# Attention scores from split queries and keys: three fp32r products in place of one float32 product

## The chip, the core and the metric

The kernel runs on one core of one Trainium2 chip. The metric is device time in microseconds (us) of one execution. The engines are named as in the profile: PE (TensorE matmuls), PEld (its weight loads), DVE (VectorE), ACT (ScalarE), POOL (GpSimd), SP (SyncE, which issues the loads).

## What is computed

A two-layer decoder trunk on 512 positions of width 1024: a state-space layer, a feed-forward layer, one attention layer with 16 heads, a second feed-forward layer, all in float32. The change touches the scores of the attention layer only. Keys and queries of a head have 96 entries (64 without and 32 with rotary position). From the reference:

```python
def causal_block_attention(q, k, v):
    ...
    scale = 1.0 / math.sqrt(dk)
    ...
        s = jnp.einsum('bhqd,bhkd->bhqk', q_blk, k).astype(jnp.float32) * scale
        query_pos = blk_idx * Q_BLOCK + jnp.arange(Q_BLOCK)
        s = jnp.where(key_pos[None, :] <= query_pos[:, None], s, NEG_INF)
        p = jax.nn.softmax(s, axis=-1).astype(v.dtype)
        return jnp.einsum('bhqk,bhkd->bhqd', p, v)
```

## The kernel before

The activations lie transposed in SBUF. Almost all matrix products are made by `mm3` (L150): each operand is a pair, a high part in the type float32r and the float32r rest, and three products (high x high L153, high x low L154, low x high L155) are summed in PSUM. `split` (L165) makes such a pair: ACT writes the high part (L168, or L171 with a scale per partition), then DVE subtracts it from the source to give the low part (L169, or L172). Weights are split in the same way (`weights`: ACT L141, DVE L142).

The attention (`attention`, L846) works on quarters of four heads. For each quarter, `open_quarter` (L859) loads and splits the weights, `proj_q` and `proj_kv` (L882, L869) project one block of 128 positions each, and `close_q` and `close_k` (L911, L908) rotate and normalise: four rotary products on DVE, a reciprocal root by eleven small DVE operations on each of two tiles, then the scaling of the queries by DVE and POOL and of the keys by POOL. The helper `tt` is recorded as L853.

For each head, `turn` (L923) transposes the queries or the keys on PE (L927) and copies the result out of PSUM by ACT with a gain per partition (L929), as plain float32 tiles `qT` and `kT` of 96 x 512. `scores` (L932) makes four blocks of 128 queries against 128, 256, 384 or 512 keys, each with one plain float32 product (L942, recorded as two matmuls with two weight loads) and one bf16 product that adds the causal mask (L943). The softmax is the row maximum on DVE (L945), the exponential with its sum on ACT (L947), the reciprocal on DVE (L948) and the scaling by DVE (widest block) or POOL (L950). `turn_p` (L954) transposes the probabilities on PE (L959) and copies them out by DVE or ACT (L964, L966), and `values` (L972) multiplies two heads by their values (L979) and splits the result.

PSUM has four banks `a` for projections and transposes (three from head 9 on), three `s` for the scores, one `po`. The program text runs the heads in a pipeline: the scores of head h+1, the transposes of head h+2 and the projections of the quarter that comes next stand beside the softmax of head h. The final order on each engine is set by a scheduler when the kernel is built (`TCARGS`, L76), from its own estimates of durations; each engine then takes its instructions in that order.

The sums of squares of the compressed latents are kept by `sumsq` (L253); its tile for the latents comes from a pool of intermediate results (L789).

Of the kernel before, what the change touches and what calls it, by code (L numbers as in the profile page):

```python
# [7 lines left out]
F32 = mybir.dt.float32  # L8
F32R = mybir.dt.float32r
BF16 = mybir.dt.bfloat16  # L10
I32 = mybir.dt.int32
AF = mybir.ActivationFunctionType
# [4 lines left out]
P = 128  # L17
D = 1024
S = 512
# [3 lines left out]
T = 4  # L23
# [55 lines left out]
def places(z):  # L79

    return z.rearrange("p (i c) -> p i c", i=T)


def by_place(z):

    return z.rearrange("p (c i) -> p i c", i=T)


class Trunk:
# [160 lines left out]

        return [self.hp.tile([P, S], F32R, name=f"{name}{x}{k}", tag=f"h{x}{k}") for x in "hl"]

    def sumsq(self, k, src=None, acc=None, n="acc", pool=None, natural=False):  # L253
        nc = self.nc
        src = self.x[:, k, :] if src is None else src
        sq = (pool or self.hp).tile([P, S], F32, name=n) if k == 0 else self.hp.tile([P, S], F32, name="sq", bufs=2)
        if natural:
            nc.scalar.activation(out=by_place(sq), in_=places(src), func=AF.Square)  # L258
        else:
            nc.scalar.activation(out=sq, in_=src, func=AF.Square)  # L260
        if k == 0:
            return sq
        nc.gpsimd.tensor_tensor(out=acc, in0=acc, in1=sq, op=ALU.add)  # L263
        return acc
# [469 lines left out]
    def mla(self):  # L734
        tc, nc, a = self.tc, self.nc, self.a
# [7 lines left out]
        with ExitStack() as st:  # L743
            self.banks(a=4, po=1, s=3)
            hs, acc = self.normed(None, "m", natural=True)
            lp = st.enter_context(tc.tile_pool(name="mlal", bufs=1))
            self.qp = st.enter_context(tc.tile_pool(name="mlaq", bufs=2))
            ip = st.enter_context(tc.tile_pool(name="mlai", bufs=1))
# [12 lines left out]
            for w in ("q", "k"):  # L761
                gn = self.s(w + "rope")
                for n, tab, half in (("c1", cs, 0), ("s2", sn, 1), ("s1", sn, 0), ("c2", cs, 1)):
                    z = lp.tile([P, 4, 16], F32, name=f"rt{w}{n}")
# [9 lines left out]
            sacc = {}  # L774
            kr_raw = ip.tile([32, S], F32, name="krraw")
            specs = [(n, m) for n, nt in (("kr", 1), ("kv", 2), ("q", 3)) for m in range(nt)]
            def project(group):
                ws = [self.weights(a["w_" + n + "_a"][m], (KD, 32 if n == "kr" else P), self.s("mix1" if n == "q" else "kvin")) for n, m in group]
                pss = [self.ps("a") for _ in group]
                self.products([ps[0:32] if n == "kr" else ps for ps, (n, m) in zip(pss, group)], ws, hs, len(group) > 1)  # L780
                for ps, (n, m) in zip(pss, group):
                    if n == "kr":
                        nc.scalar.activation(out=by_place(kr_raw), in_=places(ps[0:32]), func=AF.Copy)
                        continue
                    ch = lp.tile([P, S], F32R, name=f"{n}h{m}")
                    cl = lp.tile([P, S], F32R, name=f"{n}l{m}")
                    self.split(by_place(ch), by_place(cl), places(ps), self.s(n + "a")[:, m:m + 1])
                    low.setdefault(n, []).append((ch, cl))
                    sacc[n] = self.sumsq(m, ps, sacc.get(n), n + "acc", ip, natural=True)  # L789

            def columns(z):
                cps = self.ps("s")
# [4 lines left out]
            def factors(j, n, dim):  # L797
# [6 lines left out]
                for i, hd in ((0, 64),) if j == 0 else ((1, 64), (2, 32)):  # L804
                    v.scalar_tensor_tensor(out=tfs[:, i], in0=tf[:, j], scalar=1.0 / hd, in1=tf[:, j], op0=M_, op1=M_)

            project(specs[:2])
            project(specs[2:3])
            rs = lp.tile([P, 4], F32, name="rs")
            self.rsqrt(ip, rs, columns(acc), 1.0 / D, "r1")  # L810
# [5 lines left out]
            for z in specs[3:]:  # L816
                project([z])
# [28 lines left out]
    def attention(self, low, krot, tabs, tf, tfs, maskb, identb):  # L846
        tc, nc, a = self.tc, self.nc, self.a
# [7 lines left out]
        qp = self.qp  # L855
        os = []
        quarters, heads, outs = {}, {}, {}
# [65 lines left out]
        def turn(h, w):  # L923
            z = quarters[h // 4][3 if w == "q" else 2]
            ps = self.ps("a")
            for b in range(4):
                nc.tensor.transpose(out=ps[0:96, b * P:(b + 1) * P], in_=z[:, b, h % 4, :], identity=ident)  # L927
            o = qp.tile([96, S], F32, name=w + "T")
            nc.scalar.activation(out=o, in_=ps[0:96], func=AF.Copy, scale=self.s(w + "nope")[0:96, 0:1])  # L929
            heads[h, w] = o  # L930

        def scores(h):  # L932
            qT, kT = heads[h, "q"], heads[h, "k"]
            mx = qp.tile([P, 4], F32, name="mx")
            sm = qp.tile([P, 4], F32, name="sm")
            pbs = [None] * 4
            b2 = self.ps("s")
            for i in (0, 2, 1, 3):
                n = (i + 1) * P
                bank = b2 if i in (0, 2) else self.ps("s")  # L940
                ps = bank[:, 384:512] if i == 0 else bank[:, 0:n]
                nc.tensor.matmul(out=ps, lhsT=qT[:, i * P:n], rhs=kT[:, 0:n], start=True, stop=False)  # L942
                nc.tensor.matmul(out=ps[:, i * P:n], lhsT=identb, rhs=maskb, start=False, stop=True)  # L943
                m1, s1 = mx[:, i:i + 1], sm[:, i:i + 1]
                v.reduce_max(out=m1, in_=ps, axis=AX.X, negate=True)  # L945
                pb = qp.tile([P, n], F32, name=f"p{i}")
                nc.scalar.activation(out=pb, in_=ps, func=AF.Exp, bias=m1, accum_out=s1)  # L947
                v.reciprocal(out=s1, in_=s1)  # L948
                eng = v if i == 3 else g
                eng.tensor_scalar(out=pb, in0=pb, scalar1=s1, scalar2=None, op0=M_)  # L950
                pbs[i] = pb
            heads[h, "p"] = pbs
# [42 lines left out]
        for h in range(2):  # L995
            turn(h, "q")
            turn(h, "k")
        scores(0)
        for h in range(H):
            nq, nb = divmod(h + 7, 4)  # L1000
            if h + 1 < H:
                scores(h + 1)
            if h + 2 < H:
                turn(h + 2, "q")
# [27 lines left out]
        for m in range(KD):  # L1032
            w, ps = early[m] if m < 1 else (self.weights(a["w_o"][m], (KD, P), pieces=2 if m in (3, 4) else 1), self.ps(("", "s", "s", "a", "a", "a", "s", "a")[m]))
# [102 lines left out]
```

## Time and profile before

| | |
|---|---|
| median of 3 runs | 1246.48 us (1244.24 to 1248.38) |
| the profiled execution: its time | 1248.45 us |
| its span in the trace | 1246.7 us |
| PE busy | 1190.2 us, 95% of the span |
| DVE busy | 673.0 us, 54% |
| ACT busy | 477.9 us, 38% |
| POOL busy | 150.4 us, 12% |

Busy times of PE are overlapping records of pipelined matmuls, so a busy PE isn't a PE at its peak. What a matmul costs is read from the start of one to the start of the next. Idle time of an engine matters where another engine waits for what it does next. The attention stretch on which the change bears runs from about 699 us to 850 us of the span.

### The profile page before, as it was taken

The numbers are of one execution on the slowest core, as the hardware profiler recorded it, in microseconds if no ns is written. First come the engines' busy times: TensorE is split into PE (matmuls) and PEld (weight loads), VectorE is DVE, ScalarE is ACT, GpSimd is POOL, SyncE is SP. The second block draws the span as 40 slices with busy tenths as digits, with TensorE's granted clock in tenths as the row PEclk, the third lists the DMA queues.
The fourth block names the chain that finished last, engine by engine and source line by source line (L and its number), as shares of the span: only waits on it lengthen the run. The fifth ranks groups of instructions, "written<-read, shape, count | busy, mean of one in ns | idle before, by whom it ended". The sixth has DMA issues, their size and how long they took to land.

```text
span 1246.7 us, 17562 instructions
## 1 busy us (share of the span) xinstructions
PE 1190.2 (95%) x7160; PEld 964.3 (77%) x7160; DVE 673.0 (54%) x1185; ACT 477.9 (38%) x795; POOL 150.4 (12%) x167
## 2 busy tenths in 40 slices
PE   5978889999999999999999898999999999999998
PEld 4856677888888888888878666666888888888887
DVE  8688895456444444333337777854764444443221
ACT  5464444344333323223336666653342232232210
POOL 4400000002000000000142444342100000000000
PEclk8989899999999999999999899999999999999999
DMA  5201011333333333333232011102333333323331
GB/s 194 89 30 36 10 37 36 118 88 96 104 90 96 101 98 89 93 95 104 85 101 61 27 35 42 52 1 85 88 99 101 92 95 102 102 88 100 121 118 47
DMA packets 31904, 101.09 MB, mean 81 GB/s; under 512 B 3664, under 2 KB 4688, under 8 KB 31824
## 3 DMA queue, kind: packets, MB, share of 16 engines
q1 hardware_dynamic: 31680, 99.97, 26.1%
q8 instruction: 56, 0.92, 0.3%
q14 instruction: 24, 0.20, 0.1%
q10 hardware_dynamic: 144, 0.00, 0.0%
HBM read 97.86 MB, written 2.10 MB: 80 GB/s over the span
## 4 chain that ended last, share of the span: by engine, by line
PE 82%; DVE 13%; ACT 3%; issue 2%; POOL 1%; DMA 0%; DVEq 0%; SPq 0%; ACTq 0%
PE ps_ps L153 19%; PE ps_ps L154 19%; PE ps_ps L155 19%; PE ps_s L942 2%; PE ps_x L154 2%; PE ps_x L155 2%; PE ps_x L153 2%; PE ps_a L153 2%; PE ps_a L155 2%; PE ps_a L154 2%; DVE z L610 1%; PE ps_po L979 1%; PE ps_a L927 1%; PE ps_a L959 1%; PE ps_g L154 1%
## 5 line engine op out<-in xcount | busy, mean ns | idle before, releaser
L141 ACT ACTIVATE wh<-w 128x1024 fp32r<-128x1024 f32 (+3 forms) x193 | 191.0, 992 | 554.5 <-PE ps_ps L154 362.1
L142 DVE TENSOR_TENSOR wl<-w,wh 128x1024 fp32r<-128x1024 f32 (+3 forms) x193 | 222.2, 1152 | 213.4 <-ACT wh L141 213.2
L153 PE MATMUL ps_ps<-fh,wh 128*128 128x512 f32 x704 | 274.2, 390 | 0.0
L155 PE MATMUL ps_ps<-fh,wl 128*128 128x512 f32 x704 | 273.4, 389 | 0.0
L154 PE MATMUL ps_ps<-fl,wh 128*128 128x512 f32 x704 | 273.4, 389 | 0.0
L153 PEld LDWEIGHTS ps_ps<-fh,wh 128*128 128x128 f32 x704 | 132.1, 188 | 28.0 <-issue 0.5
L154 PEld LDWEIGHTS ps_ps<-fl,wh 128*128 128x128 f32 x704 | 132.1, 188 | 27.7 <-issue 0.5
L155 PEld LDWEIGHTS ps_ps<-fh,wl 128*128 128x128 f32 x704 | 132.1, 188 | 27.5
L153 PE MATMUL ps_ps<-ah,wh 128*128 128x512 f32 x352 | 136.9, 389 | 0.0
L154 PE MATMUL ps_ps<-al,wh 128*128 128x512 f32 x352 | 136.9, 389 | 0.0
L155 PE MATMUL ps_ps<-ah,wl 128*128 128x512 f32 x352 | 136.9, 389 | 0.0
L263 POOL TENSOR_TENSOR acc<-acc,sq 128x512 f32<-128x512 f32 x21 | 30.6, 1456 | 580.7 <-ACT sq L258 315.8
L720 DVE TENSOR_TENSOR ut<-ps_ps,rstd 128x512 f32<-128x512 f32 x44 | 30.4, 691 | 127.9 <-PE ps_ps L155 127.9
L155 PEld LDWEIGHTS ps_ps<-ah,wl 128*128 128x128 f32 x352 | 66.1, 188 | 13.8
L154 PEld LDWEIGHTS ps_ps<-al,wh 128*128 128x128 f32 x352 | 66.1, 188 | 13.7
L153 PEld LDWEIGHTS ps_ps<-ah,wh 128*128 128x128 f32 x352 | 66.1, 188 | 13.7
L717 DVE TENSOR_TENSOR gt<-ps_ps,rstd 128x512 f32<-128x512 f32 x44 | 30.4, 691 | 82.8 <-PE ps_ps L155 82.7
L950 POOL TENSOR_SCALAR p<-p,sm 128x128 f32<-128x128 f32 (+2 forms) x48 | 45.7, 955 | 68.8 <-DVE sm L948 61.4
L942 PE MATMUL ps_s<-kT,qT 96*128 96x384 f32 (+3 forms) x128 | 46.3, 465 | 1.6 <-ACT p L947 1.6
L947 ACT ACTIVATE p<-ps_s,mx 128x128 f32<-128x128 f32 (+3 forms) x64 | 33.4, 525 | 29.1 <-DVE mx L945 24.9
L168 ACT ACTIVATE ah<-ut 128x512 fp32r<-128x512 f32 x44 | 27.9, 633 | 31.3 <-DVE ut L721 31.3
L945 DVE TENSOR_REDUCE mx<-ps_s 128x1 f32<-128x128 f32 (+3 forms) x64 | 30.4, 484 | 16.5 <-PE ps_s L943 16.2
(383 smaller groups left out, 1767.7 us busy)
## 6 DMA issues: line engine op xcount, KB each, us to landing
w<-w_gu SPq DMA_DIRECT2D x88, 512.0 KB, 3.5
w<-w_down SPq DMA_DIRECT2D x32, 512.0 KB, 3.5
w<-w_glu SPq DMA_DIRECT2D x12, 512.0 KB, 3.5
w<-w_down SPq DMA_DIRECT2D x16, 384.0 KB, 3.0
w<-w_in SPq DMA_DIRECT2D x7, 512.0 KB, 4.1
w<-w_o SPq DMA_DIRECT2D x6, 512.0 KB, 3.5
x<-xT SPq DMA_DIRECT2D x8, 256.0 KB, 6.9
bc<-ssm_bc SPq DMA_DIRECT2D x8, 256.0 KB, 2.8
```

The lines of the kernel that those rows point to most:

```text
L141: nc.scalar.activation(out=wh[:, c], in_=w[:, c], func=AF.Copy)
L142: nc.vector.tensor_tensor(out=wl[:, c], in0=w[:, c], in1=wh[:, c].bitcast(F32), op=ALU.subtract)
L153: nc.tensor.matmul(out=out, lhsT=lh, rhs=rh, start=start, stop=False)
L154: nc.tensor.matmul(out=out, lhsT=lh, rhs=rl, start=False, stop=False)
L155: nc.tensor.matmul(out=out, lhsT=ll, rhs=rh, start=False, stop=stop)
L263: nc.gpsimd.tensor_tensor(out=acc, in0=acc, in1=sq, op=ALU.add)
L717: v.tensor_tensor(out=gt, in0=pss[0], in1=rstd, op=ALU.mult)
L720: v.tensor_tensor(out=ut, in0=pss[1], in1=rstd, op=ALU.mult)
L942: nc.tensor.matmul(out=ps, lhsT=qT[:, i * P:n], rhs=kT[:, 0:n], start=True, stop=False)
L945: v.reduce_max(out=m1, in_=ps, axis=AX.X, negate=True)
L947: nc.scalar.activation(out=pb, in_=ps, func=AF.Exp, bias=m1, accum_out=s1)
L950: eng.tensor_scalar(out=pb, in0=pb, scalar1=s1, scalar2=None, op0=M_)
```

## The change

Queries and keys of a head are split into float32r pairs when they are copied out of PSUM: the copy by ACT writes the high part, and a new DVE instruction writes the low part (L172). A score block is three float32r products instead of one float32 product. Each head so has four tiles of 96 x 512 instead of two. To make room, the sums of squares of the latents move from the pool of intermediate results into the buffers `pt0`, which later hold transposed probabilities.

```diff
-    def sumsq(self, k, src=None, acc=None, n="acc", pool=None, natural=False):
+    def sumsq(self, k, src=None, acc=None, n="acc", pool=None, natural=False, **kw):
...
-        sq = (pool or self.hp).tile([P, S], F32, name=n) if k == 0 else self.hp.tile([P, S], F32, name="sq", bufs=2)
+        sq = (pool or self.hp).tile([P, S], F32, name=n, **kw) if k == 0 else self.hp.tile([P, S], F32, name="sq", bufs=2)
...
-                    sacc[n] = self.sumsq(m, ps, sacc.get(n), n + "acc", ip, natural=True)
+                    sacc[n] = self.sumsq(m, ps, sacc.get(n), n + "acc", self.qp, natural=True, tag="pt0", bufs=4)
...
-            o = qp.tile([96, S], F32, name=w + "T")
-            nc.scalar.activation(out=o, in_=ps[0:96], func=AF.Copy, scale=self.s(w + "nope")[0:96, 0:1])
-            heads[h, w] = o
+            heads[h, w] = [qp.tile([96, S], F32R, name=w + "T" + x) for x in "hl"]
+            self.split(*heads[h, w], ps[0:96], self.s(w + "nope")[0:96, 0:1])
...
-                nc.tensor.matmul(out=ps, lhsT=qT[:, i * P:n], rhs=kT[:, 0:n], start=True, stop=False)
+                self.mm3(ps, [z[:, i * P:n] for z in qT], [z[:, 0:n] for z in kT], True, False)
```

The scheduler lays the attention out anew; from the old L930 on, the lines of the changed kernel are smaller by one. On PE at the opening, from the transposes of the first heads to the first score blocks, stands before (the name behind the arrow that comes last is the operand held in the array):

```order
L927 MATMUL ps_a<-ctab,Kt 96x128 x8
L927 MATMUL ps_a<-ctab,Qt 96x128 x8
L927 MATMUL ps_a<-ctab,Kt 96x128 x4
L942 MATMUL ps_s<-kT,qT 128x128
L943 LDWEIGHTS identb
L943 MATMUL ps_s<-maskb,identb 128x128
L942 MATMUL ps_s<-kT,qT 128x256
```

and in the changed kernel:

```order
L927 MATMUL ps_a<-ctab,Qt 96x128 x8
L153 MATMUL ps_s<-kTh,qTh 128x128
L154 MATMUL ps_s<-kTl,qTh 128x128
L153 MATMUL ps_s<-kTh,qTh 128x256
L154 MATMUL ps_s<-kTl,qTh 128x256
L153 MATMUL ps_s<-kTh,qTh 128x512
L154 MATMUL ps_s<-kTl,qTh 128x512
L927 MATMUL ps_a<-ctab,Kt 96x128 x4
L155 MATMUL ps_s<-kTh,qTl 128x128
L942 LDWEIGHTS identb
L942 MATMUL ps_s<-maskb,identb 128x128
```

Three blocks are begun with the products that need the high part of the queries, and the product with their low part follows after the next transposes.

On DVE at the same place, from the first maxima on, stands before:

```order
L945 TENSOR_REDUCE mx<-ps_s 128x1 x2
L948 RECIPROCAL sm<-sm 128x1
L945 TENSOR_REDUCE mx<-ps_s 128x1
L948 RECIPROCAL sm<-sm 128x1
L945 TENSOR_REDUCE mx<-ps_s 128x1
```

and in the changed kernel:

```order
L172 SCALAR_TENSOR_TENSOR kTl<-ps_a,smalls,kTh 96x512 x2
L172 SCALAR_TENSOR_TENSOR qTl<-ps_a,smalls,qTh 96x512 x2
L944 TENSOR_REDUCE mx<-ps_s 128x1 x3
L947 RECIPROCAL sm<-sm 128x1 x2
L944 TENSOR_REDUCE mx<-ps_s 128x1 x2
L947 RECIPROCAL sm<-sm 128x1
L949 TENSOR_SCALAR p_6076<-p_6076,sm 128x512
L172 SCALAR_TENSOR_TENSOR qTl<-ps_a,smalls,qTh 96x512
L944 TENSOR_REDUCE mx<-ps_s 128x1
L172 SCALAR_TENSOR_TENSOR kTl<-ps_a,smalls,kTh 96x512
```

Four low halves stand ahead of the first maximum and more of them between the softmax steps.

On DVE in the second closing of a quarter, between the split of the query weights and the start of the reciprocal roots, stands before:

```order
L853 TENSOR_TENSOR Qt<-rq_6602,rq_6603 128x16x16
L948 RECIPROCAL sm<-sm 128x1
L142 TENSOR_TENSOR wl<-w,wh 128x384
L945 TENSOR_REDUCE mx<-ps_s 128x1
L853 TENSOR_TENSOR ss<-ss,tfs 128x32
L853 TENSOR_TENSOR ss<-ss,tfs 128x16
L945 TENSOR_REDUCE mx<-ps_s 128x1 x2
L181 TENSOR_SCALAR r42x<-ss 128x32
```

and in the changed kernel:

```order
L853 TENSOR_TENSOR Qt<-rq_6678,rq_6679 128x16x16
L963 COPY pt_6801<-ps_a 128x256
L172 SCALAR_TENSOR_TENSOR qTl<-ps_a,smalls,qTh 96x512
L947 RECIPROCAL sm<-sm 128x1
L142 TENSOR_TENSOR wl<-w,wh 128x384
L944 TENSOR_REDUCE mx<-ps_s 128x1
L853 TENSOR_TENSOR ss<-ss,tfs 128x32
L172 SCALAR_TENSOR_TENSOR kTl<-ps_a,smalls,kTh 96x512
L947 RECIPROCAL sm<-sm 128x1
L853 TENSOR_TENSOR ss<-ss,tfs 128x16
L947 RECIPROCAL sm<-sm 128x1
L181 TENSOR_SCALAR r42x<-ss 128x32
```

Two low halves stand ahead of the reciprocal roots.

## Rows read from the trace of the kernel before

**Rows 1.** Busy us (instructions) by stretch, 699 to 850 us: PE, PEld, DVE, ACT, POOL; clock.

```profile
699.25:714.30 15.05, 15.01 (x75) 11.06 (x76) 8.22 (x25) 11.64 (x29) 6.81 (x7) 0.87 0.00 1
714.30:731.20 16.90, 15.79 (x86) 10.91 (x84) 16.89 (x59) 10.99 (x29) 6.88 (x9) 1.00 0.23 66
731.20:755.80 24.60, 22.98 (x133) 17.76 (x133) 12.95 (x37) 15.98 (x38) 11.77 (x12) 0.93 0.01 1
755.80:771.90 16.10, 14.12 (x78) 9.81 (x77) 16.10 (x58) 10.41 (x26) 7.14 (x9) 1.00 0.24 78
771.90:791.80 19.90, 18.68 (x117) 13.96 (x116) 11.42 (x32) 13.81 (x33) 9.45 (x10) 1.00 0.01 1
791.80:809.10 17.30, 15.70 (x78) 10.55 (x77) 16.86 (x58) 10.36 (x24) 6.36 (x7) 0.90 0.26 93
809.10:850.00 40.90, 39.28 (x230) 27.45 (x230) 20.18 (x55) 20.43 (x52) 16.27 (x16) 1.00 0.00 1
```

**Rows 2.** Timeline of PE behind two closings: start us, us, what, [idle before <-releaser].

```profile
732.15 0.64 PE L927 MATMUL ps_a<-ctab,Qt 128*96 128x128 f32 x4 [1.15 <-POOL Qt L853]
...
774.73 0.53 PE L927 MATMUL ps_a<-ctab,Kt 128*96 128x128 f32 x3 [1.22 <-POOL Kt L853]
```

**Rows 3.** Timeline of PE: score blocks of 384, 256, 512, 128 columns and their masks.

```profile
741.73 0.81 PE L942 MATMUL ps_s<-kT,qT 96*128 96x384 f32 x2
742.38 0.22 PE L943 MATMUL ps_s<-maskb,identb 128*128 128x128 bf16 x1
...
743.98 0.60 PE L942 MATMUL ps_s<-kT,qT 96*128 96x256 f32 x2
744.42 0.22 PE L943 MATMUL ps_s<-maskb,identb 128*128 128x128 bf16 x1
744.48 1.07 PE L942 MATMUL ps_s<-kT,qT 96*128 96x512 f32 x2
745.39 0.22 PE L943 MATMUL ps_s<-maskb,identb 128*128 128x128 bf16 x1
...
746.10 0.39 PE L942 MATMUL ps_s<-kT,qT 96*128 96x128 f32 x2
746.32 0.22 PE L943 MATMUL ps_s<-maskb,identb 128*128 128x128 bf16 x1
```

**Rows 4.** Timeline of PE: split products, three steps each of 384 and 512 columns.

```profile
752.67 0.34 PE L155 MATMUL ps_a<-wh,ql 128*128 128x384 f32 x1
...
753.20 0.34 PE L155 MATMUL ps_a<-wh,ql 128*128 128x384 f32 x1
...
754.14 0.40 PE L154 MATMUL ps_a<-wl,kvh 128*128 128x512 f32 x1
...
754.83 0.39 PE L154 MATMUL ps_a<-wl,kvh 128*128 128x512 f32 x1
```

**Rows 5.** Timeline of PEld: the two weight loads of one score block.

```profile
744.42 0.30 PEld L942 LDWEIGHTS ps_s<-kT,qT 96*128 96x128 f32 x2
```

**Rows 6.** Mask products (PE, PEld) by stretch: those of the three closings.

```profile
714.30:731.20 16.90, 1.33 (x6) 0.58 (x6) 1.00 0.23 66
...
755.80:771.90 16.10, 1.26 (x6) 0.48 (x5) 1.00 0.24 78
...
791.80:809.10 17.30, 1.80 (x8) 0.89 (x8) 0.90 0.26 93
```

**Rows 7.** DVE prices: line L172 (ns min/median/max), and a group of L717.

```profile
L172 DVE SCALAR_TENSOR_TENSOR fl<-x,smalls,fh x16: 737/744/1793, 273.1 to 887.0; 128x512 fp32r<-128x512 f32 x16
...
L172 DVE SCALAR_TENSOR_TENSOR ql<-ps_a,smalls,qh x3: 1135/1144/1160, 661.4 to 672.6; 128x512 fp32r<-128x512 f32 x3
...
L717 DVE TENSOR_TENSOR gt<-ps_ps,rstd 128x512 f32<-128x512 f32 x44 | 30.4, 691 | 82.8 <-PE ps_ps L155 82.7
```

**Rows 8.** Timeline of DVE at the opening: its first maximum.

```profile
702.62 0.29 DVE L945 TENSOR_REDUCE mx<-ps_s 128x1 f32<-128x128 f32 x1 [3.48 <-PE ps_s L943]
```

**Rows 9.** Groups of DVE, 640 to 880 us: the low halves of the values.

```profile
L169 DVE TENSOR_TENSOR ol<-ps_po,oh 128x512 fp32r<-128x512 f32 x8 | 8.5, 1058 | 7.5 <-ACT oh L168 7.5
```

## Prediction

> **What bounds the kernel now.** I read the page first, then the stretch that the change touches, cut at the moments when the vector engine (DVE) starts and ends the closing of a quarter of the heads [rows 1]. Outside 699 to 850 us nothing moves: the order of instructions on TensorE (PE), ScalarE (ACT) and DVE is the same before the first score product and after the last one. Inside, two engines take turns at the end of the waits. In four of the seven stretches PE is busy nearly throughout (15.01 of 15.05 us, 22.98 of 24.60, 18.68 of 19.90, 39.28 of 40.90) and DVE has room. In the other three, 50.3 us together, DVE is busy for 16.89 of 16.90, 16.10 of 16.10 and 16.86 of 17.30 us. There it splits the weights of the next quarter, rotates and scales its queries, and does the softmax work of running heads in between. What these stretches hold up can be seen on PE: its next transposes start after 1.15 us of idleness that POOL's scaling of the queries ends, and after 1.22 us that POOL's scaling of the keys ends [rows 2]; both scalings wait for factors that DVE makes at the end of its stretch. So a PE saving is worth its price in the first kind of stretch and little in the second, where each instruction added to DVE costs its whole length.
>
> **TensorE: what three products save.** The records of a matmul overlap, so I take starts. A plain float32 score block is two records; from its start to the start of its mask product it takes 0.22, 0.44, 0.65 and 0.91 us for 128, 256, 384 and 512 columns [rows 3], 2.22 us a head. Products of split operands (fp32r) of the projections follow each other in steps of 0.53/3 = 0.177 us at 384 columns and 0.69/3 = 0.230 us at 512 [rows 4]. Three of them make 0.53 and 0.69 us. For 256 columns no row exists; the straight line through the two gives 0.124, so 0.37 for three. For 128 columns the line gives 0.071, but the second weight load of a score block starts 0.11 us after the first (two loads of 0.19 us lie within 0.30) [rows 5], and a product can hardly follow faster than its load; I take 3 x 0.11 = 0.33. Sum 1.92 us a head, a saving of 0.30, or 0.075 a block, and 4.8 us over 16 heads. Bounds: with 0.071 at 128 columns 6.7 us saved; with each narrow product as slow as a whole plain float32 block of that width (0.22, so 0.66 for three) 0.5 us lost.
>
> Of the 64 blocks 6 + 6 + 8 = 20 lie in the three DVE stretches [rows 6]. Their 1.5 us buy nothing, since DVE ends those stretches. The other 44 give 44 x 0.075 = **3.3 us**.
>
> [...]
>
> **VectorE: what the low halves add.** `turn` now ends in `split`: ACT's copy with scale stays as it was, with an fp32r output, and costs nothing new; behind it DVE computes the low half, 32 new instructions of 96x512 out of PSUM. No row has this shape. The nearest are the same operation from SBUF (0.744 us median), a DVE operation of 512 columns from PSUM in plain order (0.691), and the same operation from PSUM in permuted order (1.144) [rows 7]. The access here is plain, so I take 0.72, between the first two, with 0.69 and 1.14 as ends: 23.0 us of DVE work (22 to 37) into 150.8 us of which DVE now fills 102.6 (the seven of [rows 1] added).
>
> Where they stand decides. The order of the changed program puts 7 of the 32 into the opening, 1, 2 and 1 into the three closings (from the first weight split to the scaling of the queries), and the rest into stretches with room. The 4 in the closings cost 4 x 0.72 = **2.9 us**. More softmax work is drawn into the second closing as well (3 more maxima, 1 more scaling); that is work moved ahead from the next stretch, where DVE fills 11.42 of 19.90 us, and I count it as nothing. Of the 7 in the opening the first four fall into 3.48 us in which DVE had nothing to do [rows 8]; the other three, 2.2 us, stand in a stretch that is not full (8.22 of 15.05), between softmax steps. Bounds 0 and 2.2, I take the middle, **1.1 us**. The 21 others cost nothing: their cover is the 40.9 us by which DVE falls short of filling the other three PE stretches [rows 1], and a transpose that comes two heads ahead of its scores; without that cover each would cost 0.72.
>
> Edits at no cost: the sums of squares of the latents now live in a buffer of the ring that later holds transposed probabilities. They are read last before the attention begins, so the ring is free by then. The bank of a transposed head stays taken for 0.72 us longer; four banks (three from head 9 on) rotate, and the cover is the same as above. POOL keeps its instructions; in the third closing it now scales the keys ahead of the queries, and since PE transposes both next, I count nothing.
>
> **Sum:** -3.3 + 2.9 + 1.1 = +0.7 us on the profiled execution, 1248.45 us. That execution was 2.0 us over the median of the three runs; a run from the middle of them gives 1246.48 + 0.7 = 1247.2. About 0.3%, 3.7 us, is what a measurement of this kernel tells from no change, so this counts as the same.
>
> **Rivals.** (1) The PE saving comes through whole. For it: the closings hold softmax work that PE doesn't wait for, so new DVE work could push only that back. Against: the three stretches are filled to the last 0.4 us [rows 1] and PE idles at the end of two. Price -4.8: 1241.7.
>
> (2) Slower: DVE stands still inside its queue. It takes its instructions in order, so a low half that reaches the head of the queue before ACT has written the high half holds up all maxima, reciprocals and copies behind it, and PE behind these. The value splits show it: in front of 8 of them DVE sat idle 7.5 us for ACT [rows 9], 0.94 us for each. If the new ones in the closings and the last three of the opening wait as long, 7 x 0.94 = 6.6 us come on top: 1253.8. It decides from a mean wait of about 0.43 us, where these seven take 3.0 us and the total passes the 3.7. Against: the order was laid out with ACT's time in it, and the queue holds other work ahead of most of them.
>
> (3) Slower: narrow products run at the plain float32 rate, 0.22 us each at 128 columns. No product of split operands narrower than 384 columns is in this trace, so nothing excludes it. Then a head costs 2.25 us on PE, none is saved, and the 3.3 us fall out of the sum: +4.0, 1250.5.
>
> [...]
>
> **How the numbers follow.** My forecast, DVE takes back what PE gives, has 0.52. Its own range, from the bounds of the opening and of 256 and 128 columns and from a DVE price up to 1.14 in the closings, is 1244 to 1250.5; I leave 0.02 of it under -3.7 and 0.08 over +3.7. Rival 1 has 0.20, rival 2 0.18, rival 3 0.10. Faster: 0.20 + 0.02 = 0.22. Same: 0.42. Slower: 0.08 + 0.18 + 0.10 = 0.36. The range reaches from 1 us under rival 1 to 2 us over rival 2, since runs of one kernel spread by some 2 us: 1240.5 to 1255.5.
>
> **What would show it.** PE: 192 score products in place of 128 records, about 0.33 us from the first product of a 128-column block to its mask, 0.69 at 512, and the masks unchanged. DVE: 32 new rows near 0.72 us on the split's line, and some 125 us busy in the stretch in place of 102.6. The three closings should be 0.7, 1.4 and 0.7 us longer between the same two instructions, still without gaps on DVE, and the last 40.9 us shorter by about 1.3. Idle time of DVE in front of the new rows, released by ACT's high half and over 10 us in sum, would be rival 2; 0.66 us for three narrow products would be rival 3; closings of unchanged length would be rival 1. The forecast is wrong if the stretch from the first head's transposes to the last values changes by more than 3.7 us either way.

## The result and the profile after

The changed kernel takes 1254.41 us (median of 8 runs, 1249.71 to 1255.64), the kernel before 1246.03 (median of 8). The ratio on record is 1.0061, with a 95% interval of 1.0046 to 1.0076: 7.6 us slower, 5.7 to 9.5 (the two medians lie 8.4 apart, the figure from which the expectations below start). The forecast range of 1240.5 to 1255.5 holds the median, but the case that I called the likeliest, no difference within 3.7 us, is not what came. Ratios below are turned into us with 1246.

The profiled execution has a span of 1253.5 us against 1246.7. Its attention begins 2.8 us earlier than before's, in code that is the same, so attention alone has grown by 9.6 us in this execution. The first view is busy time by stretch, cut at the same instructions as [rows 1]; columns: window, its length, PE, PEld, DVE, ACT, POOL busy (instructions), granted clock of PE as a share, DMA share, GB/s.

```profile
695.48:715.76 20.28, 18.04 (x83) 14.54 (x84) 13.75 (x36) 12.63 (x30) 7.16 (x8) 0.68 0.00 1
715.76:733.32 17.56, 15.76 (x95) 11.89 (x93) 17.48 (x60) 11.94 (x30) 8.41 (x10) 1.00 0.21 64
733.32:754.67 21.35, 20.14 (x127) 16.75 (x128) 15.26 (x38) 12.97 (x31) 9.24 (x10) 0.92 0.00 1
754.67:773.51 18.84, 17.06 (x102) 12.42 (x101) 18.84 (x66) 13.27 (x34) 10.62 (x11) 1.00 0.19 67
773.51:796.26 22.75, 21.68 (x142) 17.05 (x143) 17.15 (x44) 16.13 (x40) 11.09 (x12) 1.00 0.01 1
796.26:815.82 19.56, 13.57 (x82) 9.13 (x80) 19.44 (x58) 9.21 (x21) 10.33 (x8) 0.96 0.23 81
815.82:856.85 41.03, 38.68 (x228) 28.36 (x230) 22.68 (x57) 18.39 (x46) 12.75 (x13) 0.94 0.00 1
```

The opening of before, cut as exactly (at the end of the queries' scaling):

```profile
698.25:714.30 16.05, 15.01 (x75) 11.06 (x76) 9.11 (x29) 12.25 (x31) 7.76 (x8) 0.84 0.01 2
```

Read it against [rows 1]. The opening is 4.2 us longer. Its granted clock is 0.68. The records of both traces are at 1.00 or 0.50, so 13.0 of 20.28 us are at 0.50, where before it was 5.1 of 16.05. The first closing is 0.7 us longer, which is the forecast figure (n_in_after below shows that it isn't the forecast's reason); the second 2.7 instead of 1.4; the third, with the last stretch, 2.4. The three PE stretches together have hardly changed: -3.2, +2.9 and what the last has in that 2.4. The 3.3 us of PE saving are not to be seen. Added up from these rows, the whole attention of the changed kernel has some 23 us at 0.50 and before's some 12. Products of 512 columns of the changed kernel follow each other in 0.43 us there (710.24 and 710.67) and in 0.22 at 1.00 (705.40 and 705.62). By these steps, an estimate, 11 us more at 0.50 are worth up to 5.5 of the 9.6 us where PE is what a stretch waits for.

The new rows of DVE (groups by line and shape: busy, mean ns | idle of DVE ahead of them):

```profile
L172 DVE SCALAR_TENSOR_TENSOR qTl<-ps_a,smalls,qTh 96x512 fp32r<-96x512 f32 x16 | 11.9, 742 | 6.0 <-ACT qTh L171 5.8
...
L172 DVE SCALAR_TENSOR_TENSOR kTl<-ps_a,smalls,kTh 96x512 fp32r<-96x512 f32 x16 | 11.7, 739 | 1.8 <-ACT kTh L171 1.8
```

So 0.74 us each, where I took 0.72 [rows 7], and 7.8 us of DVE idle ahead of them, 7.6 of it for ACT's high half. The largest idle time of PE stands behind the third closing. PE, POOL and DVE there (timelines: start, us, what, [idle before]):

```profile
816.78 2.80 PE L927 MATMUL ps_a<-ctab,Qt 128*96 128x128 f32 x12 [4.08 <-POOL Qt L853]
```

```profile
812.84 1.90 POOL L853 TENSOR_TENSOR Kt<-Kt,sc 128x1024 f32<-128x1024 f32 x1 [0.74 <-DVE sc L853]
814.70 2.03 POOL L853 TENSOR_TENSOR Qt<-Qt,sc 128x512 f32<-128x512 f32 x1
```

```profile
812.87 2.95 DVE L853 TENSOR_TENSOR Qt<-Qt,sc 128x1024 f32<-128x1024 f32 x1
```

POOL scales the keys first, PE asks for the queries first and idles 4.08 us. That is the swap that I had counted as nothing.

### The profile page after: what moved, and what is told of

Same layout as the page of the kernel before. It is cut to its first block, busy times and chain, and to the rows that moved or that the text cites. A ratio compares the mean times of both kernels' runs of the same rounds, so it can differ in the third digit from the quotient of the medians.

```text
span 1253.5 us, 17733 instructions
## 1 busy us (share of the span) xinstructions
PE 1191.9 (95%) x7224; PEld 972.9 (78%) x7224; DVE 696.6 (56%) x1217; ACT 478.8 (38%) x795; POOL 152.9 (12%) x167
## 4 chain that ended last, share of the span: by engine, by line
PE 81%; DVE 13%; ACT 3%; issue 2%; POOL 1%; DMA 0%; DVEq 0%; SPq 0%; ACTq 0%
PE ps_ps L155 19%; PE ps_ps L153 19%; PE ps_ps L154 19%; PE ps_x L154 2%; PE ps_x L155 2%; PE ps_x L153 2%; PE ps_a L153 2%; PE ps_a L155 2%; PE ps_a L154 2%; DVE z L610 1%; PE ps_po L978 1%; PE ps_a L927 1%; PE ps_s L153 1%; PE ps_s L154 1%; PE ps_g L153 1%
## 5 line engine op out<-in xcount | busy, mean ns | idle before, releaser
L142 DVE TENSOR_TENSOR wl<-w,wh 128x1024 fp32r<-128x1024 f32 (+3 forms) x193 | 225.5, 1170 | 212.4 <-ACT wh L141 212.2
L717 DVE TENSOR_TENSOR gt<-ps_ps,rstd 128x512 f32<-128x512 f32 x44 | 30.4, 691 | 83.1 <-PE ps_ps L155 83.1
L949 POOL TENSOR_SCALAR p<-p,sm 128x128 f32<-128x128 f32 (+2 forms) x48 | 49.1, 1027 | 77.7 <-DVE sm L947 66.4
L153 PE MATMUL ps_x<-zh,wh 128*128 128x512 f32 x96 | 37.3, 389 | 0.0
L154 PE MATMUL ps_x<-zl,wh 128*128 128x512 f32 x96 | 37.3, 389 | 0.0
```

Source lines behind the costliest of these rows:

```text
L142: nc.vector.tensor_tensor(out=wl[:, c], in0=w[:, c], in1=wh[:, c].bitcast(F32), op=ALU.subtract)
L153: nc.tensor.matmul(out=out, lhsT=lh, rhs=rh, start=start, stop=False)
L154: nc.tensor.matmul(out=out, lhsT=lh, rhs=rl, start=False, stop=False)
L717: v.tensor_tensor(out=gt, in0=pss[0], in1=rstd, op=ALU.mult)
```

## First experiments: the swap, the vector work, the closings, the products

**Theory A:** the swap on POOL in the third closing makes most of the loss. **Theory B:** the vector engine's new work does, wherever it stands. **Theory C:** the opening and its half clock (0.50) do.

**a_q3**, the swap undone by an edge of order (`tt` and `scaled` now also return their instruction; the dots inside the call stand for the kind of the edge):

```diff
-            scaled(quarters[qt][2], 0, 64, scales(qt, (0,))[:, 0], g)
+            sc = scales(qt, (0,))
+            k = scaled(quarters[qt][2], 0, 64, sc[:, 0], g)
+            if qt == 3:
+                tc.add_manual_dep(k.ins, quarters[qt, "q"].ins.name, ..., reason="order")
...
-            scaled(Qt, 64, 96, sc[:, 1], g)
+            quarters[qt, "q"] = scaled(Qt, 64, 96, sc[:, 1], g)
```

> The changed kernel with one more edge of order: on POOL the keys' scaling of the last quarter stays behind the queries' scaling, as in the kernel before. Up to the third closing its order is that of the changed kernel. Theory A (the swap on POOL in the third closing made most of the loss): TensorE's 4.1 us of idleness in front of the last quarter's transposes falls by about 1.9 us, the length of the keys' scaling, and of the 6.8 us at half clock behind it half or all goes, worth 1.7 to 3.4 us more: 1249 to 1252.5 us. Theory B (the vector engine's new work makes the loss, wherever it stands): 1254, unchanged within 1 us. Theory C (the opening and its half clock make most of it): no more than 1.9 us gained, 1252.5 or more, with the opening still near 20.3 us.

Measured: ratio 1.0064 [1.0041, 1.0086], +8.0 us, no gain. The repair works where it was made. Timelines of PE, POOL and DVE:

```profile
815.05 2.80 PE L930 MATMUL ps_a<-ctab,Qt 128*96 128x128 f32 x12 [2.35 <-POOL Qt L853]
...
834.54 0.46 PE L153 MATMUL ps_s<-kTh,qTh 96*128 96x384 f32 x1 [0.87 <-ACT p L949]
```

```profile
812.91 2.08 POOL L853 TENSOR_TENSOR Qt<-Qt,sc 128x512 f32<-128x512 f32 x1 [0.82 <-DVE sc L853]
```

```profile
812.87 1.22 DVE L853 TENSOR_TENSOR Qt<-Qt,sc 128x1024 f32<-128x1024 f32 x1
```

PE starts the transposes 1.73 us earlier and DVE's scaling takes 1.22 us again. But behind it the scheduler has laid the softmax work in another order, PE waits 0.87 us for an exponential, its clock is 0.83 between 830 and 840 us where the changed kernel has 1.00, and the last stretch is 42.54 us long instead of 41.03. Of the 1.71 us by which the third closing is shorter (17.85 against 19.56), the last stretch gives back 1.51. Theory A falls as the main cause.

**b_low**, the vector work alone: the kernel before, with

```diff
+            lo = qp.tile([96, S], F32R, name=w + "Tl")
+            nc.vector.scalar_tensor_tensor(out=lo, in0=ps[0:96], scalar=self.s(w + "nope")[0:96, 0:1], in1=o, op0=M_, op1=S_)
```

> The kernel before with the 32 low halves computed on VectorE and read by nobody (their tiles and the moved sum of squares included); the score products stay plain float32. The price of the vector work alone. Theory B: 8.4 us of loss plus the TensorE saving that the changed kernel has and this one hasn't, 3 to 5 us: 1257 to 1260. Theory A: the queries stay ahead of the keys on POOL here, so only what the prediction counted, 2.9 in the closings and 1.1 in the opening: about 1250. Theory C: the opening as long as in the changed kernel (20 us) only if the vector work makes it so; if the half clock there comes from the order of the products, the opening stays near 16 us.

Measured: 1.0052 [1.0032, 1.0071], +6.5 us. More than A allowed, less than B. The opening is 18.76 us long at a clock of 0.77, so the vector work, with the order that the scheduler laid for it, lengthens it without the products.

**s_close**, three heads left plain, so that no low half stands in a closing:

```diff
+            if h in (3, 7, 11):
+                o = qp.tile([96, S], F32, name=w + "Tp", tag=w + "Th")
+                nc.scalar.activation(out=o, in_=ps[0:96], func=AF.Copy, scale=self.s(w + "nope")[0:96, 0:1])
+                heads[h, w] = o
+                return
...
+                if h in (3, 7, 11):
+                    nc.tensor.matmul(out=ps, lhsT=qT[:, i * P:n], rhs=kT[:, 0:n], start=True, stop=False)
```

> The changed kernel with heads 3, 7 and 11, whose low halves stand in the closings, left at the plain float32 product; 13 heads are split. No low half is left in a closing, and POOL has the queries ahead of the keys in the third. Theory B: the 2.9 us of the closings go and 0.9 us of TensorE saving with them: about 1252. Theory A: the swap is gone as well, so 1246 to 1249. Theory C: the opening stays at 20 us, so 1250 or more whatever happens in the closings.

Measured: 1.0047 [1.0028, 1.0065], +5.9 us. That is 1.7 us under the changed kernel, with intervals of some 2 us on either side. B's count comes to 2.0 (2.9 less 0.9), and C stands too: the opening is 20.38 us long at a clock of 0.68. A, which wanted 5 to 8 us back, falls a second time (POOL has the queries first here).

**a_nolow**, the products alone:

```diff
-            heads[h, w] = [qp.tile([96, S], F32R, name=w + "T" + x) for x in "hl"]
-            self.split(*heads[h, w], ps[0:96], self.s(w + "nope")[0:96, 0:1])
+            o = qp.tile([96, S], F32R, name=w + "Th")
+            nc.scalar.activation(out=o, in_=ps[0:96], func=AF.Copy, scale=self.s(w + "nope")[0:96, 0:1])
+            heads[h, w] = [o, o]
```

> The changed kernel without the low halves: the three products take the high tile in place of the low one, so the low parts are left out of the scores and VectorE has none of its 32 new instructions. TensorE's part alone. Prediction's prices: 3.3 us saved outside the closings up to 4.8 with all: 1241 to 1243. Narrow products in steps of 0.06 us as the trace of the changed kernel has them: up to 6.7, 1239.5. Theory C, if the opening's half clock comes from the products and not from the vector work: the opening still at 20 us and the time at 1246 or more.

Measured: 1.0024 [1.0014, 1.0034], 3.0 us **slower** than before, although PE has less to do and DVE nothing new. Its opening is 15.81 us, so this isn't theory C. None of the three theories explains it. What else is different is the order: the scheduler has other durations to plan with and lays the whole attention anew. It did so for b_low and s_close as well, so the figures of this group hold work and order together.

## Second experiments: the order held fixed

To part the order from the lengths I wrote orders out by hand. A wrapper keeps every instruction that the attention gives to PE, DVE, ACT and POOL, and a list chains them:

```diff
+            made, plain = [], self.nc
+            self.nc = Rec(plain, made)
             self.attention(low, krot, tabs, tf, tfs, maskb, identb)
+            self.nc = plain
+            ORDER = {
+                'tensor': ...
...
+                for x, y in zip(at, at[1:]):
+                    tc.add_manual_dep(mine[y], mine[x].name, ..., reason="order")
```

In the profiles of these kernels all rows of the attention have the wrapper's line, so tiles tell them apart. **Theory D:** the new order is the price. **Theory E:** what PE saves turns into waits in any order.

**o_nolow** is a_nolow in the order of before, three products where one score product stood.

> The kernel without low halves of the first group (three products, the high tile in place of the low one, low parts left out), with PE, DVE, ACT and POOL held by a written-out list to the order of the kernel before: every instruction of the attention stands where its counterpart stood, three products where one score product stood. Against the kernel before only the length of the score products differs. Theory D (the price of TensorE's part is the new order that the scheduler lays for other lengths): the saving of 3.3 to 4.8 us appears, so some 4 us under the kernel before and 6 to 7 under the same kernel in its own order. Theory E (what TensorE saves turns into waits for the softmax steps in any order): as long as the kernel before within 1 us, or longer.

Measured: 0.9983 [0.9968, 0.9998], 2.1 us **faster** than before (0.2 to 4.0), 5.1 under the same kernel in its own order. In the traces DVE, ACT and POOL run the same sequence of instructions as in the kernel before. By stretch, as above:

```profile
698.41:713.75 15.34, 14.22 (x85) 11.93 (x86) 9.13 (x29) 12.23 (x30) 7.59 (x8) 0.89 0.01 2
713.75:730.69 16.94, 15.65 (x92) 11.55 (x90) 16.94 (x59) 11.07 (x29) 6.88 (x9) 1.00 0.23 67
730.69:754.94 24.25, 22.50 (x144) 18.85 (x144) 13.02 (x37) 15.97 (x38) 11.78 (x12) 0.93 0.00 1
754.94:771.06 16.12, 13.93 (x82) 10.48 (x83) 16.12 (x58) 10.37 (x26) 7.17 (x9) 1.00 0.27 78
771.06:790.51 19.45, 18.16 (x125) 14.61 (x124) 11.05 (x30) 13.79 (x33) 9.59 (x10) 1.00 0.01 2
790.51:809.63 19.12, 17.26 (x87) 11.95 (x86) 17.07 (x59) 10.45 (x24) 6.58 (x7) 0.82 0.25 83
809.63:849.63 40.00, 38.11 (x244) 28.69 (x244) 19.75 (x55) 20.48 (x52) 16.20 (x16) 1.00 0.00 1
```

The three PE stretches are 1.7 us shorter than before's (83.7 against 85.4), at the same clocks. No run holds the kernel before to its own order by such a list, so a small price of the list itself is not excluded.

**b_in_nolow** is the kernel before in the order of a_nolow.

> The other way round: the kernel before, plain float32 score products and all, held to the order that the scheduler laid for the kernel without low halves. Theory D: slower than the kernel before by the price of that order, the 2.7 us by which the kernel without low halves was over it plus the 3.3 to 4.8 of saving: 6 to 7.5 us. Theory E: order doesn't matter, so within 1 us of the kernel before.

Measured: 1.0023 [1.0011, 1.0035], +2.9 us with nothing changed but the order. Theory D holds, at half its price for the plain kernel. It is lost in the three PE stretches, which are 2.8 us longer (88.2 against 85.4), behind closings of the same length, 50.3 us. One reading is that PE work which had lain beside full closings now stands behind them: PE's busy time in the closings is 45.6 us before [rows 1] and 43.3 in b_in_nolow (14.74, 14.69, 13.85). But 1.9 of these 2.3 us are in the third closing, where before ran at a clock of 0.90, 3.5 us at 0.50, and b_in_nolow at 1.00; by the steps of 0.43 and 0.22 us above, that alone could make 1.7 us of busy time. How much work moved is open.

**o_after** is the changed kernel, whole, in the order of before.

> The changed kernel, whole, held to the order of the kernel before; each of the 32 low halves is put into DVE's order 0.3 us after the end of ACT's high half in the trace of the kernel before. Eight low halves then stand in the opening, and 1, 1 and 2 in the closings. Theory D: the prediction's sum holds with the order undisturbed, +0.7 us against the kernel before, and 7 under the changed kernel. Theory B (the vector engine's 23.6 us make the loss in any order): 6 us over the kernel before, less up to 4.8 of saving: +1.5 to +6. If it stays at +8, neither order nor lengths explain the loss and the score path through the new operation does.

Measured: 1.0117 [1.0087, 1.0146], +14.6 us. All three numbers of the expectation were too small. With the low halves in, the scheduler's new order is 7.0 us cheaper than the old one, into which I had put them by one rule for all 32. In that old order they cost 14.6 + 2.1 = 16.7 us, 0.52 each, where I had let 21 of them go free.

**o_room** splits only the ten heads whose low halves stand neither in the opening nor in a closing.

> Heads 4, 5, 6, 8, 9, 10 and 12 to 15 with split products, heads 0 to 3, 7 and 11, whose low halves stand in the opening or in a closing, with plain float32 products, held to the order of the kernel before. Theory D: ten heads save 0.30 us each on TensorE and no low half stands where the vector engine ends the stretch: 2 to 3 us under the kernel before. Theory B: 20 low halves of 0.74 us at 6/32 us each make +3.8, less 3: +1. Theory E: +3 to +4.

Measured: 1.0029 [1.0019, 1.0039], +3.6 us. With the 1.3 us that ten heads save on PE (10/16 of 2.1), twenty low halves in stretches with room cost 4.9 us. Its trace says how (timelines of PE in the three PE stretches: the rows that waited for a low half):

```profile
730.80 0.66 PE L1078 MATMUL ps_a<-ctab,p 128*128 128x128 f32 x4 [1.45 <-DVE qTl L1078]
...
733.45 0.33 PE L1078 MATMUL ps_s<-kTl,qTh 96*128 96x128 f32 x1 [0.46 <-DVE kTl L1078]
```

```profile
773.64 0.33 PE L1078 MATMUL ps_s<-kTl,qTh 96*128 96x128 f32 x1 [1.21 <-DVE kTl L1078]
```

```profile
810.36 1.35 PE L1078 MATMUL ps_a<-ctab,Kt 128*96 128x128 f32 x8 [0.91 <-DVE qTl L1078]
...
812.53 0.33 PE L1078 MATMUL ps_s<-kTl,qTh 96*128 96x128 f32 x1 [0.46 <-DVE kTl L1078]
...
823.40 0.39 PE L1078 MATMUL ps_s<-kTl,qTh 96*128 96x256 f32 x1 [0.69 <-DVE kTl L1078]
...
828.64 0.64 PE L1078 MATMUL ps_a<-ctab,Kt 128*96 128x128 f32 x4 [0.59 <-DVE qTl L1078]
```

Two kinds of wait. Score products wait for their operand kTl: 0.46 + 1.21 + 0.46 + 0.69 = 2.8 us. Transposes into ps_a, of probabilities or keys, wait for a bank that qTl still reads: 1.45 + 0.91 + 0.59 = 3.0 us, of which o_nolow has 0.9, there for ACT's copy. Together 4.9 us more than in o_nolow. The three PE stretches are 5.2 us longer than there (88.9 against 83.7), although one of o_nolow's ran at a clock of 0.93 and these at 1.00. Its closings are 2.1 us shorter (50.1 against 52.2): o_nolow's third took 19.12 us at a clock of 0.82, this one 17.01 at 1.00. So the two attentions as a whole differ by 3.1 us only.

## Third experiments: which low halves, and which wait

**Theory G:** the loss in the PE stretches stands where a quarter begins. **o_late** and **o_first** divide o_room's heads, in the order of before: 5, 6, 9, 10, 13, 14, 15, and 4, 8, 12.

> In the order of the kernel before, heads 5, 6, 9, 10, 13, 14 and 15 with split products; the others, among them 4, 8 and 12, with which a quarter begins, with plain float32 products. Theory G (the low half costs where a quarter begins: products, and transposes that need the bank, stand waiting for it, with nothing else to do): these seven heads save 0.2 to 0.3 us each on TensorE and wait some 1 us in all: 1 us under the kernel before, between -2 and 0. Theory B (each low half costs its share wherever it stands, 6 us over 32 low halves): 14 of them 2.6 us, less 2.1: about +0.5 to +1.

> The complement: in the order of the kernel before, only heads 4, 8 and 12 with split products, six low halves. Theory G: the waits that the twenty-low-half kernel's trace shows at these three places, 1.9, 1.2 to 1.9 and 1.4 us, less 0.9 saved: 3 to 4 us over the kernel before. Theory B: 6 x 0.19 less 0.9: no difference, within 0.5 us.

Measured: o_first 1.0036 [1.0020, 1.0051], +4.5 us with six low halves, as theory G had it and not as B (no difference). o_late 1.0020 [1.0005, 1.0034], +2.5 us, where G wanted -2 to 0 and B up to 1. The trace of o_first has G's waits: 2.4 us for banks that qTl still reads, 1.7 us for kTl. G is right on the first heads and incomplete: the later heads pay in the last stretch. The prices don't add, though: the two kernels lose 7.0 us together, o_room, which has both sets of heads, 3.6, so a price per head isn't to be had from them. PE there in o_late:

```profile
809.15 0.64 PE L1078 MATMUL ps_a<-ctab,Kt 128*96 128x128 f32 x4 [0.96 <-DVE qTl L1078]
...
820.76 0.38 PE L1078 MATMUL ps_s<-kTl,qTh 96*128 96x256 f32 x1 [0.69 <-DVE kTl L1078]
...
826.00 0.64 PE L1078 MATMUL ps_a<-ctab,Kt 128*96 128x128 f32 x4 [0.59 <-DVE qTl L1078]
```

2.2 us, and two of the three are waits for a bank: from head 9 on the program has three banks `a` instead of four.

**o_unread** computes all 32 low halves as o_after does, but no product waits for one:

```diff
-                self.mm3(ps, [z[:, i * P:n] for z in qT], [z[:, 0:n] for z in kT], True, False)
+                self.mm3(ps, [z[:, i * P:n] for z in (qT[0], qT[0])], [z[:, 0:n] for z in (kT[0], kT[0])], True, False)
```

> All 32 low halves computed as in the changed kernel held to the order of before, but the products take the high tile in their place, so the low parts are left out of the scores. TensorE waits for a low half now only where a transpose needs its bank. If the loss of 13.6 us of that kernel lies in products that wait for their operand, some 3 to 4 us of it go (the kTl waits of its trace are 0.8, 0.5, 1.2 and 1.1): +10. If it lies in DVE's queue and the banks, it stays: +12.5 to +14.

Measured: 1.0074 [1.0052, 1.0096], +9.2 us. 5.4 us of o_after's loss, with an uncertainty of some 4.5, hang on the operand, and the 3.6 us of kTl waits are within that; 11.3 us over o_nolow stay with DVE's queue, the banks and the opening (20.04 us, as in o_after).

**n_in_after** takes the 32 low halves out of the changed kernel and holds its order.

> The changed kernel without its 32 low halves (the products take the high tile in their place, so the low parts are left out of the scores), held to the order that the scheduler laid for the changed kernel, on POOL in the third closing too. Against the changed kernel only the low halves differ, against the three-product kernel in the order of before only the order. If the low halves themselves make the loss (waits at the start of a quarter, banks, the full closings), most of the 8.4 us goes: 1246 to 1249 with before at 1246. If the order that was laid for them makes it, little goes: 1252 to 1254.

Measured: 1.0036 [1.0022, 1.0051], +4.5 us: between the two expectations, 3.1 us under the changed kernel and 6.6 over o_nolow. By stretch, as above:

```profile
698.33:715.35 17.02, 15.36 (x83) 12.58 (x84) 9.13 (x30) 12.23 (x30) 7.62 (x8) 0.80 0.01 1
715.35:732.88 17.53, 15.76 (x95) 11.88 (x93) 16.80 (x59) 12.06 (x30) 8.25 (x10) 1.00 0.21 65
732.88:752.79 19.91, 18.72 (x127) 15.29 (x128) 11.41 (x32) 12.85 (x31) 9.21 (x10) 1.00 0.00 1
752.79:771.30 18.51, 16.81 (x102) 12.48 (x101) 17.66 (x64) 13.32 (x34) 10.55 (x11) 1.00 0.22 68
771.30:793.74 22.44, 21.39 (x142) 17.00 (x143) 12.67 (x37) 16.36 (x40) 11.34 (x12) 1.00 0.01 1
793.74:812.95 19.21, 13.78 (x82) 9.40 (x80) 18.54 (x57) 9.14 (x21) 8.01 (x8) 0.88 0.26 83
812.95:853.81 40.86, 38.42 (x228) 28.91 (x230) 17.70 (x49) 18.46 (x46) 12.72 (x13) 0.93 0.00 1
```

The closings are 55.3 us long without a single low half, 50.3 before: DVE does more softmax steps inside them (64 instructions in the second instead of 58), and the third has the swap (3.73 us of PE idle in this trace too). The three PE stretches behind them give little back, 83.2 us against o_nolow's 83.7. And the opening: same order as the changed kernel, 17.02 us at a clock of 0.80 (6.8 us at 0.50) against 20.28 at 0.68 (13.0). The low halves there cost 3.3 us, and by the steps of 512 columns above 6.2 us more at 0.50 are worth 3.1: by this estimate nearly all of it is clock. About 3.4 of the 6.2 are a second spell at 0.50, from about 708.4 to 711.8 us (granted clock 1.00 from 705.5 to 707.5, 0.50 from 708.5 to 711.5). What PE did ahead of it, in the changed kernel:

```profile
707.04 0.44 PE L958 MATMUL ps_a<-ctab,p 128*128 128x128 f32 x2 [0.37 <-DVE qTl L172]
...
708.30 0.52 PE L154 MATMUL ps_s<-kTl,qTh 96*128 96x256 f32 x1 [0.70 <-DVE kTl L172]
```

It stood still twice, 0.37 and 0.70 us, and the granted clock went from 1.00 to 0.50 about when the second wait ended; whether the waits have to do with it is not shown. The other 2.8 us are a first spell that lasts longer, in which PE, after 1.73 us of idleness for POOL's scaling of the queries, is busy throughout in both kernels; no run shows why. These two rows are also most of what PE waits for low halves in the whole attention of the changed kernel: 1.3 us, 0.9 for kTl and 0.4 for a bank that qTl reads.

So the 7.6 us are made of three parts, by the runs: the products alone **-2.1**, the order that the scheduler laid **+6.6**, the 32 low halves in that order **+3.1**. The intervals of two ratios go into each difference, so the last two are good to some 2.5 us, and which of them is the larger is not settled. The profiled executions, attention alone (the rows above added up), give -0.5, +4.3 and +5.9 of 9.6 us. Nor is this the only way to cut it: by o_after the low halves in the old order cost +16.7 and the new order gives 7.0 back. The order was laid for the low halves, and the two have no prices of their own. What holds either way is that the products alone lose nothing, and that the new order without low halves, and the low halves in either order, each lose.

The two parts look different on PE. From o_nolow to n_in_after, the order, PE's idle time in the attention grows from 11.4 to 15.2 us and its busy time by 0.4. From there to the changed kernel, the low halves, idle time grows by 1.2 us, to 16.4, and PE is busy 4.7 us longer on the same instructions in the same order, with some 23 us at 0.50 instead of some 17, worth 3 by the same estimate; the other 1.7 is not explained. So in the order that the scheduler laid, the low halves cost little by PE waiting for them; more of their price goes with the granted clock, and what lowers that is open.

## Why the prediction was right or wrong

**TensorE's saving, mis-sized.** The term of 4.8 us whole, 3.3 outside the closings, measured 2.1 (0.2 to 4.0). The traces of o_nolow and of the kernel before agree: over the 48 blocks that neither a wait nor a granted clock of 0.50 touches in either, 2.3 us are saved, 0.048 a block where I had 0.075, and 44 of these make 2.1. The steps of 0.177 and 0.230 us that I took are there, and a 128-column product follows in 0.11, in some blocks in 0.06 (805.20 and 805.26 us), so that a product can hardly follow faster than its load, at 0.11, is not shown. But behind another kind of product the first product of a block takes longer. Two blocks of the changed kernel on PE:

```profile
746.45 0.31 PE L153 MATMUL ps_s<-kTh,qTh 96*128 96x128 f32 x1
746.59 0.28 PE L154 MATMUL ps_s<-kTl,qTh 96*128 96x128 f32 x1
746.70 0.27 PE L155 MATMUL ps_s<-kTh,qTl 96*128 96x128 f32 x1
746.82 0.23 PE L942 MATMUL ps_s<-maskb,identb 128*128 128x128 bf16 x1
...
750.79 0.42 PE L153 MATMUL ps_s<-kTh,qTh 96*128 96x384 f32 x1
751.05 0.34 PE L154 MATMUL ps_s<-kTl,qTh 96*128 96x384 f32 x1
751.23 0.33 PE L155 MATMUL ps_s<-kTh,qTl 96*128 96x384 f32 x1
751.40 0.23 PE L942 MATMUL ps_s<-maskb,identb 128*128 128x128 bf16 x1
```

0.26 for the first of 384 columns, 0.18 and 0.17 for the next. So a block takes 0.37 and 0.61 where I had 0.33 and 0.53, and the narrowest block is dearer than the plain one, 0.22 [rows 3]. The trace of before had this step already, in the first split product behind a mask, 0.26 us:

```profile
742.41 0.42 PE L153 MATMUL ps_a<-wh,qh 128*128 128x384 f32 x1
742.67 0.34 PE L154 MATMUL ps_a<-wl,qh 128*128 128x384 f32 x1
```

Rival 3 (0.66 for three narrow products) is refuted as well. In the block of 384 columns above the second and third product follow in 0.26 and 0.18 us and the mask in 0.17, and each of the three brings a weight load of 0.19 (PEld, from 750.77, 750.88 and 751.05 us).

**The low halves in the closings: right in price where the order stays, luck in the changed kernel.** One more low half in a closing that keeps its order makes it 0.6 to 0.7 us longer (o_after against o_nolow: 17.58 and 16.94, 16.79 and 16.12). In the changed kernel the first closing is 0.7 us longer as forecast, but n_in_after has it at 17.53 us without a low half, against 17.56: there DVE has room (16.80 of 17.53), and the low half fits in. All four low halves add 0.7 us to the three closings (56.0 against 55.3), not 2.9; without them the closings are already 5.0 us longer than before's. What failed is the sentence on the softmax work drawn into the second closing, "I count it as nothing": n_in_after has that work without low halves, and its second closing is 18.51 us, 2.4 over before.

**"The 21 others cost nothing": the reason failed.** I took 40.9 us of free DVE time as their cover. The cover of a low half isn't the free time of its engine but what its consumer has left to do. At the start of a quarter the scores come straight behind the transposes, not two heads later, and PE, held to the old order, has nothing else: o_first pays 4.5 us for six of them. In the order that the scheduler laid PE hardly waits for them: the three PE stretches of the changed kernel are 1.9 us longer than n_in_after's (85.1 against 83.2), with 0.2 us of waits for low halves behind the opening, so there the term was off by 1.9 us at most, part of it clock. The sentence on PSUM, that the bank stays taken 0.72 us longer under the same cover, failed with it in the old order: in o_room 2.1 us more of PE's waits are for a bank. In the changed kernel it is 0.4 us.

**The opening, mis-sized.** 1.1 us, bounds 0 to 2.2, from DVE's free time; 4.2 in the profile, 3.3 of them by the low halves in the same order, nearly all of that, by the estimate above, at the lower clock. The granted clock was in no bound.

**The swap on POOL: the reason failed, the number didn't matter.** PE transposes the queries first, so it does wait, 4.08 us; undone, 1.73 of them went, and the end stayed (a_q3).

**What the sum left out.** I read the new order from its rows, counted low halves in it, and gave the order itself no price. Without low halves it costs 6.6 us by the runs, 4.3 by the profiles, mostly in the closings (55.3 us, against o_nolow's 52.2 and before's 50.3). This is the step of the forecast that failed: "DVE takes back what PE gives", +0.7 us and the same, had the saving, the low halves and nothing else in its sum. Rival 1 (the saving whole) is refuted. Rival 2 came nearest with 1253.8, by a mechanism that isn't shown: DVE idles ahead of low halves for ACT, 7.6 us in all, below the 10 us that I had set. In the old order what waits is PE for the low half itself rather than the softmax behind it. That the closings have no gaps on DVE was right to about 0.1 us; that the last stretch is 1.3 us shorter was wrong. The range held by luck: its upper end came from rival 2, while the forecast's own range, 1244 to 1250.5, missed.

No version that computes the low halves beats the kernel before: the best, o_late, which splits seven heads, is 2.5 us over it.

## What to carry to other kernels

An instruction that is put between two engines is covered by what its consumer, and whoever wants its buffer next, still has to do, not by the free time of its own engine: look for the places where a pipeline starts, and where buffers are fewest. The runs in the old order show this (o_first, +4.5 us for six low halves). Where a scheduler lays the order from durations, a change of durations is a change of order, and that can cost more than the change: here 2.9 us for the plain kernel, 5.1 and 6.6 for the one with three products. Holding an order by hand parts the two, but only for the kernel that is held: with the low halves in, the new order was the cheaper one. A stretch that comes out at the forecast length proves nothing of the reason; the first closing did so without the instruction that was to lengthen it. A saving that stands in four pieces per head has to be priced with the first piece behind another kind of product (here 0.26 us at 384 columns), not with the steady step (0.17).

## What the runs showed of the hardware

DVE's scaling of 128 x 1024 takes 1.22 us when it starts 0.04 us before POOL's scaling of the queries (a_q3), and 2.95 when it starts 0.03 us after POOL's scaling of the keys (the changed kernel; 2.96 in n_in_after, 0.02 us after). In the changed kernel 1.87 us of POOL's 1.90 were left when DVE started, and 2.95 is 1.73 more than 1.22; what the two have in common is not shown.

Of the eight runs of the changed kernel the one with the shortest span, 1247.9 us, has a mean granted clock of 0.985 and the one with the longest, 1253.7, one of 0.978. In the profiles of all these kernels the part behind the attention takes the same 396.7 us, the part ahead of it, in code that is the same, 693.2 to 699.3.
